# Norms in two steps, the pooling tied behind the mixing, and the recurrence's scans spread over the LRU gate

## The chip, the cores and the metric

The program runs on one core of a Trainium2 chip. The metric is the device time of one execution in microseconds (us): the time before is the median of three runs, 1450.72 us (1448.88 to 1451.69). The engines are TensorE (PE), VectorE (DVE), ScalarE (ACT), GpSimd (POOL) and SyncE (SP). Each works through its own instructions strictly in their order; semaphores tie the engines together.

## The reference

A batch of one, 256 tokens by 1024 features, float32, goes through two blocks. The first has two layers; each merges three branches of one input projection: a gated MLP with a spatial mix, an attention with low-rank queries and keys, and a gated linear recurrence (RG-LRU, 1280 channels). The second block has a pooling mixer and then a sparse attention, each followed by a convolutional FFN (2816 wide) and a gated per-layer embedding (PLE). What matters here:

```python
# RG-LRU, in each layer of the first block
a = jnp.exp(-8.0 * r * softplus(-lam))              # r, i: sigmoid gates of the convolved input xc
mult = jnp.sqrt(jnp.maximum(1.0 - a * a, 0.0))
h = scan(a, mult * i * xc)                          # h[t] = a[t]*h[t-1] + b[t] along the 256 tokens
y_c = h * silu(z_c)
merged = (sigmoid(g_a) * (y_a @ w_proj_a) + sigmoid(g_b) * (y_b @ w_proj_b)
          + sigmoid(g_c) * (y_c @ w_proj_c))
x = x + rmsnorm(merged @ w_out, post_norm_g)        # the next layer starts with rmsnorm(x)
# second block, layer 0
x = x + pool_mixer(rmsnorm(x), pool_w, pool_scale)  # average over the last 2, 4, 8, 16 tokens, minus the token, times a matrix
x = x + conv_ffn(rmsnorm(x))
x = x + sigmoid(rmsnorm(x) @ ple_gate) * (p @ ple_proj)   # then the norms for keys and values, attention, FFN, PLE
```

## The kernel before, in words

**Weights.** All weights are streamed once, in a fixed order, in chunks of up to 128x1024 floats: SP's queue loads a chunk into `raw` (4 buffers), ScalarE copies it, rounded to fp32r, into `hi` (L376), VectorE subtracts to get the remainder `lo` (L379, two instructions of 128x512), and TensorE multiplies. A product of two split operands is three matmuls, `mm3` (L481, L482, L483): in the rows `psA<-hi,hT` is weight chunk hi with the split input hT. There are 7 buffers of hi and lo, and a chunk is split two chunks ahead of its use in the program.

**Tokens.** They lie as two halves of 128 partitions, `x[0]` and `x[1]` (`x_70`, `x_71` in the rows), each 128x1024. A norm (`norm`, L543) sums squares of the two 512-wide quarters on ScalarE (`junk`, L512), adds them on VectorE (`ms`, L501), takes the power -1/2 on GpSimd (`rs`, L502), scales the quarters on VectorE (`tmp`, L526), or first multiplies by the gain where the factor is folded in later, transposes on TensorE (L538, into psB) and splits the transposed tile on ScalarE (hi, L488) and VectorE (lo, L489) into `hT`, the input of the next matrix. TensorE can't start the next matrix before that.

**The LRU gate.** In `first_layer` the recurrence's coefficients `av` are done, on ScalarE, before the branch gate `gc` is computed (two column halves n, four chunks each, from L894). The block from L982 to L994 then squares av (L985), takes the minimum with 1 (L986), the root on ScalarE (L987, with its own table), multiplies (L989) and scans along the tokens (L992). The next matrix is zc: five pairs, each one gated into `yc` (L1001, L491, L492), then the matrix pc, which reads yc.

**The residuals.** `tok_pair` (L579) multiplies both halves with the 8 chunks of a 1024x1024 matrix (wo here, pg in `ple`): six chunks are held, so that half 0 ends before half 1 does. Only after the whole call does the program write the residual and the norm of half 0 and then of half 1; for wo (L1012 to L1020) `t` is the product times a gain, and x gets t times rs. `ffn` does the same behind its `down` matrix. `pool` (L1071) averages with a matrix `pm` in psB (`pooled`, L1089), splits into `uf`, and mixes (`mixed`, L1096).

**Order.** The program is written engine by engine in the order of these Python calls; a list scheduler with costs of its own then fixes the order of each engine, by the readiness that it computes, and adds semaphore waits. That order doesn't change at run time.

Of the kernel before, what the change touches and what calls it, by code (L numbers as in the profile page):

```python
# [12 lines left out]
AF = mybir.ActivationFunctionType  # L13
ALU = mybir.AluOpType
AX = mybir.AxisListType

P = 128
S = 256
D = 1024
KD = D // P  # L20
# [16 lines left out]
KF = D_FF // P  # L37
# [148 lines left out]
FFN_LAG = 8  # L186
NSA_ORDER = (("kv", 1), ("kv", 2), ("q", 0), ("cmp", 0), ("cmp", 1), ("gt", 0))
FFN_TAIL = 7
PAIR_HELD = 6
SPECS = _specs()  # L190
W_TOTAL = sum(n for _, n, _ in SPECS) * P
# [227 lines left out]
class Net:  # L419
# [59 lines left out]
    def mm3(self, ps, a, b, start, stop):  # L479
        mm = self.nc.tensor.matmul  # L480
        mm(ps, a[0], b[0], start=start, stop=False)  # L481
        mm(ps, a[0], b[1], start=False, stop=False)  # L482
        mm(ps, a[1], b[0], start=False, stop=stop)  # L483

    def split(self, hi, lo, src, scale=None):
        nc = self.nc
# [56 lines left out]
    def norm(self, *key, dst=None, rs=None, fold=None):  # L543


        gain = self.row(*key)
        dst = dst or self.feat4("hT", KD)
        run_rs = rs or [None, None]

        def run(half):  # L550
            if fold:
                hs = self.u2s("h", 2)
                for n, h in enumerate(hs):
                    cs = slice(n * 512, (n + 1) * 512)
                    self.nc.vector.tensor_tensor(h, self.x[half][:, cs], gain[n], op=ALU.mult)
            if run_rs[half] is None:
                run_rs[half] = self.rs_x(half, fold or 1.0)
            if not fold:
                hs = self.scaled_x(half, run_rs[half], gain)
            for n, h in enumerate(hs):  # L560
                self.transpose_split(h, dst, half, 4 * n, 4)

        run.dst, self.rs = dst, run_rs
        return run

# [10 lines left out]
                self.mm3(ps[half][:, :N], f.pair(kg, half), (wh[:, k, :], wl[:, k, :]), kg == 0, kg == kts - 1)  # L576
            yield ps[half]

    def tok_pair(self, key, f):  # L579

        ps = [[self.psA(), self.psA()] for _ in range(2)]
        def part(half, i, w):
            n, c = divmod(i, 4)
            for k in range(2):
                kg = 2 * c + k
                self.mm3(ps[n][half], f.pair(kg, half), (w[0][:, k, :], w[1][:, k, :]), kg == 0, kg == KD - 1)

        def get(i):
            return self.w.get((*key, i // 4, i % 4), 512)

        ws = [get(i) for i in range(PAIR_HELD)]
        for i in range(PAIR_HELD):
            part(0, i, ws[i])
        for i in range(8 - PAIR_HELD):
            part(1, i, ws[i])
            ws.append(get(PAIR_HELD + i))
            part(0, PAIR_HELD + i, ws[-1])
        for i in range(8 - PAIR_HELD, 8):
            part(1, i, ws[i])
        return ps  # L600

    def feat_tile(self, ps, key, f, kts=KD, k0=0, tot=None):
# [130 lines left out]
    def first_layer(self, l):  # L733
# [241 lines left out]
        for kind, i in MERGE_ORDER:  # L975
            if kind == "a":
                project("pa", i, ya, 8, gate("ga", i))
            else:
                gates(i)
        tg = [gate("gc", n) for n in range(2)]  # L980
        tv = self.u2s("tv", 5)
        quarter = self.small(1, "quarter", 2)  # L982
        nc.vector.tensor_scalar(quarter, av[4][:, :1], 0.0, 0.25, op0=ALU.mult, op1=ALU.add)
        for j in range(5):
            nc.vector.tensor_tensor(tv[j], av[j], av[j], op=ALU.mult)  # L985
            nc.vector.tensor_scalar(tv[j], tv[j], 1.0, None, op0=ALU.min)  # L986
            nc.scalar.activation(tv[j], tv[j], AF.Sqrt, bias=quarter, scale=-0.25)  # L987
        for j in range(5):
            nc.vector.tensor_tensor(xc[j], xc[j], tv[j], op=ALU.mult)  # L989
            for e in range(2):  # L990
                ct = 2 * j + e
                nc.vector.tensor_tensor_scan(ctile(av, ct), ctile(av, ct), ctile(xc, ct), 0.0,  # L992
                                             op0=ALU.mult, op1=ALU.add)
        if l == 1:  # L994
            self.ple_load(0)
            self.w.scale = self.row("pscale")
        yc = self.feat2("yc", KL)
        for j in range(5):
            sz = self.tmp()
            self.silu2(sz, self.feat_pair(("zc", l), hT, j))  # L1000
            nc.vector.tensor_tensor(sz, av[j], sz, op=ALU.mult)  # L1001
            self.split(*yc.span(2 * j, 2), _k3(sz, S), 0.5)

# [5 lines left out]
                self.transpose_split(merged[half][n], ms, half, 4 * n, 4, 0.5)  # L1009
        g_post = self.row("post", l)  # L1010
        nxt = self.norm("pre", 1) if l == 0 else self.pool_norm()
        pss = self.tok_pair(("wo", l), ms)  # L1012
        for half in range(2):
            ts = self.u2s("t", 2)
            for n in range(2):
                nc.vector.tensor_tensor(ts[n], pss[n][half], g_post[n], op=ALU.mult)
            r = self.rs_of([pss[0][half], pss[1][half]], D)
            for n in range(2):
                xs = self.x[half][:, n * 512:(n + 1) * 512]
                nc.vector.scalar_tensor_tensor(xs, ts[n], r, xs, op0=ALU.mult, op1=ALU.add)  # L1020
            nxt(half)
        self.hT = nxt.dst

    def mla_head(self, h, qT, kT, qrT, krT, vt, szb, yb):
# [46 lines left out]
    def pool(self):  # L1071
        nc = self.nc
        h = self.hT
        pms = [self.sp.tile([P, 1024], F32, tag=t, name="pm", bufs=HL_BUFS) for t in ("hi", "lo")]
        for i in range(2):
            nc.scalar.dma_start(pms[i], self.aps["pm"][:, i * 1024:(i + 1) * 1024])
        pm = [p.rearrange("p (g k t) -> p g k t", g=2, k=2) for p in pms]
        self.ple_in(0, 0)
        self.rope_tables()
        w = [self.w.get(("pool", gp), S) for gp in range(2)]  # L1080
        nxt = self.norm("ffn", 0)
        uf = self.feat4("uf", 8)
# [12 lines left out]

        def mixed(half):  # L1096
            for gp in range(2):
                wh, wl = w[gp]
                cs = slice(gp * 512, gp * 512 + 512)
                ps = self.psA()  # L1100
                for e in range(2):
                    for k in range(2):
                        self.mm3(ps[:, e * S:(e + 1) * S], uf.pair(4 * gp + 2 * e + k, half),
                                 (wh[:, 2 * e + k, :], wl[:, 2 * e + k, :]), k == 0, k == 1)
                nc.vector.tensor_tensor(self.x[half][:, cs], self.x[half][:, cs], ps, op=ALU.add)

        pooled(0, 0)
        pooled(1, 0)
        mixed(0)
        pooled(1, 1)  # L1110
        nxt(0)
        mixed(1)
        nxt(1)
        self.hT = nxt.dst

    def ffn(self, l):
# [5 lines left out]
        act = {}  # L1122

        def up(j):
# [16 lines left out]
            self.split(f[:, 0, :], f[:, 1, :], c[:, :S])  # L1141
            act[j] = f

        def down(*js):
            ws = [self.w.get(("down", l, j), 512) for j in js]
            for half in range(2):
                sl = slice(half * P, half * P + P)
                for j, (wh, wl) in zip(js, ws):
                    f = act[j]
                    for n in range(2):  # L1150
                        self.mm3(acc[half][n], (f[:, 0, sl], f[:, 1, sl]), (wh[:, n, :], wl[:, n, :]),
                                 j == 0, j == KF - 1)

        for j in range(KF):
            up(j)
# [2 lines left out]
        for j in range(KF - FFN_LAG, KF - FFN_TAIL):  # L1158
            down(j)
        nxt = self.norm("ple", l, fold=0.5)  # L1160
        down(*range(KF - FFN_TAIL, KF))
        for half in range(2):
            for n in range(2):
                cs = slice(n * 512, (n + 1) * 512)
                nc.vector.tensor_tensor(self.x[half][:, cs], self.x[half][:, cs], acc[half][n], op=ALU.add)  # L1165
            nxt(half)
        self.hT = nxt.dst

    def ple_load(self, l):
# [14 lines left out]
    def ple(self, l):  # L1184
        nc = self.nc
        hT, rs = self.hT, self.rs
        if l == 0:
            self.ple_load(1)
        nxt = self.norm("nkv", fold=1.0) if l == 0 else self.final()
        pss = self.tok_pair(("pg", l), hT)  # L1190
        for half in range(2):
            for n in range(2):
                cs = slice(n * 512, n * 512 + 512)
                t = self.tmp()
                nc.scalar.activation(t, pss[n][half], AF.Tanh, scale=rs[half])
                nc.vector.scalar_tensor_tensor(t, t, 1.0, self.pp[half][n], op0=ALU.add, op1=ALU.mult)
                nc.vector.tensor_tensor(self.x[half][:, cs], self.x[half][:, cs], t, op=ALU.add)
            nxt(half)
        self.hT = nxt.dst

    def rope_nsa(self, x, tab, nh, n):
# [331 lines left out]
```

## Time and profile before

| | us |
|---|---|
| median of 3 runs | 1450.72 |
| profiled execution | 1449.2 |
| its span in the trace | 1447.4 |
| TensorE busy | 1406.5 (97%) |
| VectorE busy | 1059.7 (73%) |
| ScalarE busy | 842.0 (58%) |
| GpSimd busy | 73.2 (5%) |

The span is that of the trace; the execution has 1.8 us more around it. The share of TensorE, 97%, is a mean: it is nearly 100% within the matrices, and lower where the program goes from one matrix to the next through a norm or a gate. The mean granted clock of TensorE is 0.996 of full speed. A matmul's own duration in a row is longer than the distance to the next one, since they are pipelined.

### The profile page before, as it was taken

How to read it: one execution, taken by the hardware profiler on the slowest of the kernel's cores; microseconds unless marked ns; L12 is line 12 of the kernel's file. 1: busy time of each engine (PE TensorE's matmuls, PEld its weight loads, DVE VectorE, ACT ScalarE, POOL GpSimd, SP SyncE). 2: the span in 40 equal slices, each digit the busy share in tenths (PEclk: the TensorE clock that was granted, in tenths of full speed). 3: DMA queues.
4: the chain of work that ended last, by engine and by line, in shares of the span. 5: the costliest groups of instructions: out<-in, count | busy, mean ns of one | idle time of the engine just before them, and what ended most of it. 6: DMA issues, size and time to landing. Idle time of an engine off the chain costs nothing.

```text
span 1447.4 us, 23030 instructions
## 1 busy us (share of the span) xinstructions
PE 1406.5 (97%) x8522; PEld 1235.7 (85%) x8522; DVE 1059.7 (73%) x2163; ACT 842.0 (58%) x1411; POOL 73.2 (5%) x118
## 2 busy tenths in 40 slices
PE   6999999999999999999999999999999999999997
PEld 6987889889789878898897899999778677999986
DVE  7856748659677567486597788776795888787765
ACT  6665545656465665456564566554665786665553
POOL 1000002100010000021000000000100120000000
PEclk9999999999999999999999999999999999999999
DMA  8563456554655634555656455555453106655552
GB/s 281 182 195 117 166 183 196 170 202 149 218 161 195 197 117 159 190 187 170 211 178 218 150 201 178 190 186 193 167 181 131 59 15 191 194 184 189 187 162 90
DMA packets 73408, 249.32 MB, mean 172 GB/s; under 512 B 8272, under 2 KB 8912, under 8 KB 73296
## 3 DMA queue, kind: packets, MB, share of 16 engines
q1 hardware_dynamic: 72576, 245.95, 51.9%
q10 hardware_dynamic: 720, 1.91, 0.4%
q8 instruction: 67, 1.10, 0.3%
q14 instruction: 45, 0.37, 0.1%
HBM read 246.77 MB, written 1.05 MB: 171 GB/s over the span
## 4 chain that ended last, share of the span: by engine, by line
PE 81%; DVE 9%; DMA 4%; ACT 3%; issue 2%; POOL 1%; POOLq 0%; ACTq 0%; DVEq 0%; SPq 0%
PE psA L481 22%; PE psA L482 22%; PE psA L483 22%; DMA raw<-in_w_dram 3%; PE psB L481 3%; PE psB L482 3%; PE psB L483 3%; DVE lo L379 3%; ACT hi L376 2%; PE psB L538 1%; DVE av L992 1%; POOL rs L502 1%; PE psB L1036 1%; PE psB L1054 1%; PE psB L1422 1%
## 5 line engine op out<-in xcount | busy, mean ns | idle before, releaser
L379 DVE TENSOR_TENSOR lo<-raw,hi 128x512 fp32r<-128x512 f32 (+2 forms) x897 | 583.9, 677 | 217.4 <-ACT hi L376 212.0
L376 ACT ACTIVATE hi<-raw 128x1024 fp32r<-128x1024 f32 (+3 forms) x449 | 466.7, 1044 | 310.6 <-PE psA L483 110.3
L482 PE MATMUL psA<-hT,hi 128*128 128x256 f32 x1160 | 328.6, 283 | 0.5 <-DVE hT L489 0.5
L483 PE MATMUL psA<-hT,lo 128*128 128x256 f32 x1160 | 328.2, 283 | 0.0
L481 PE MATMUL psA<-hT,hi 128*128 128x256 f32 x1160 | 328.2, 283 | 0.0
L481 PE MATMUL psA<-hi,hT 128*128 128x512 f32 (+2 forms) x592 | 230.5, 390 | 3.9 <-ACT hT L488 3.9
L482 PE MATMUL psA<-lo,hT 128*128 128x512 f32 (+2 forms) x592 | 228.6, 386 | 1.6 <-DVE lo L379 1.6
L483 PE MATMUL psA<-hi,hT 128*128 128x512 f32 (+2 forms) x592 | 229.1, 388 | 0.0
L482 PEld LDWEIGHTS psA<-hT,hi 128*128 128x128 f32 x1160 | 221.9, 191 | 2.0 <-DVE hT L489 0.7
L481 PEld LDWEIGHTS psA<-hT,hi 128*128 128x128 f32 x1160 | 221.8, 191 | 1.5 <-ACT hT L488 0.2
L483 PEld LDWEIGHTS psA<-hT,lo 128*128 128x128 f32 x1160 | 222.0, 191 | 0.0
L481 PEld LDWEIGHTS psA<-hi,hT 128*128 128x128 f32 x592 | 111.5, 188 | 24.1 <-ACT hT L488 4.9
L482 PEld LDWEIGHTS psA<-lo,hT 128*128 128x128 f32 x592 | 111.4, 188 | 21.9 <-DVE lo L379 2.3
L483 PEld LDWEIGHTS psA<-hi,hT 128*128 128x128 f32 x592 | 111.4, 188 | 20.6 <-DVE hT L489 0.7
L1135 DVE SCALAR_TENSOR_TENSOR tmp<-psA,colt,tmp 128x255 f32<-128x255 f32 (+1 forms) x176 | 84.1, 478 | 1.2
L502 POOL TENSOR_TENSOR rs<-ms,mhalf 128x1 f32<-128x1 f32 x34 | 28.9, 851 | 979.2 <-DVE ms L501 790.6
L481 PE MATMUL psB<-hi,fact 128*128 128x512 f32 x176 | 68.8, 391 | 0.0
L482 PE MATMUL psB<-lo,fact 128*128 128x512 f32 x176 | 68.8, 391 | 0.0
L483 PE MATMUL psB<-hi,fact 128*128 128x512 f32 x176 | 68.5, 389 | 0.0
L1132 ACT ACTIVATE tmp<-psA,colt 128x256 f32<-128x256 f32 x88 | 48.5, 551 | 1.9
L512 ACT ACTIVATE junk<-x 128x512 bf16<-128x512 f32 x36 | 22.6, 628 | 36.3 <-DVE x L1165 14.0
L936 POOL CAST es<-xs 64x256 fp32r<-64x256 f32 x48 | 29.4, 640 | 270.1 <-ACT xs L488 269.3
(343 smaller groups left out, 2235.0 us busy)
## 6 DMA issues: line engine op xcount, KB each, us to landing
raw<-in_w_dram SPq DMA_DIRECT2D x414, 512.0 KB, 3.7
raw<-in_w_dram SPq DMA_DIRECT2D x24, 384.0 KB, 3.9
row<-in_rows_dram SPq DMA_DIRECT2D x34, 256.0 KB, 5.6
raw<-in_w_dram SPq DMA_DIRECT2D x8, 448.0 KB, 3.2
raw<-in_w_dram SPq DMA_DIRECT2D x4, 480.0 KB, 3.3
x<-in_x_dram SPq DMA_DIRECT2D x4, 256.0 KB, 4.6
pm<-in_pm_dram ACTq DMA_DIRECT2D x2, 512.0 KB, 5.3
out_dram<-h SPq DMA_DIRECT2D x4, 256.0 KB, 2.1
```

The source lines that it names most:

```text
L376: self.nc.scalar.activation(hi[:, :n], t[:, :n], AF.Copy)
L379: self.nc.vector.tensor_tensor(lo[:, c], t[:, c], hi[:, c].bitcast(F32), op=ALU.subtract)
L481: mm(ps, a[0], b[0], start=start, stop=False)
L482: mm(ps, a[0], b[1], start=False, stop=False)
L483: mm(ps, a[1], b[0], start=False, stop=stop)
L502: nc.gpsimd.tensor_tensor(rs, ms, self.mhalf, op=ALU.pow)
L512: nc.scalar.activation(junk[:, :s.shape[1]], s, AF.Square, scale=float(n) ** -0.5 / mul, accum_out=ss[:, i:i + 1])
L538: nc.tensor.transpose(ps[:, i, :], src[:, (done + i) * P:(done + i + 1) * P], self.cf("ident"))
L936: nc.gpsimd.tensor_copy(edges[p][m][i][r], xs.pair(ct)[i][r].bitcast(F32))
L992: nc.vector.tensor_tensor_scan(ctile(av, ct), ctile(av, ct), ctile(xc, ct), 0.0, op0=ALU.mult, op1=ALU.add)
L1132: nc.scalar.activation(dst, src, AF.Identity, bias=self.col("fb", ct, l), scale=self.col("fw", 2 * 2 * KF + ct, l))
L1135: nc.vector.scalar_tensor_tensor(dst[:, s:], src[:, :S - s], self.col("fw", (2 - s) * 2 * KF + ct, l), dst[:, s:], op0=ALU.mult, op1=ALU.add)
```

## The change

Five edits. (1) At the LRU gate the squares go from VectorE to ScalarE, the minimum from VectorE to GpSimd, and the five steps of multiply and scan are called one by one: j=0 after the first half of gate gc, j=1 after the second, j=2 to 4 inside the first three pairs of zc. (2) A norm's `run` is cut into `scale` (sums, rs, scaled quarters) and `turn` (transposes and split), and callers place the two. (3) `tok_pair` calls the residual of half 0 before half 1's last chunks; for pg the transposes of half 0 are tied, by `issue_after`, behind the fourth of half 1's last six chunks; for wo in layer 0 both `turn` calls come after the whole matrix. (4) In `pool` the pooling of half 1 is tied behind the last product of the mixing of half 0, and half 0's transposes behind the mixing of half 1. (5) In `ffn` half 0's transposes are tied behind the third last j of half 1's down products. Line numbers after the change are 2 higher up to `split`, and 19 to 53 higher from `first_layer` to `ple`.

```diff
@@ norm
-        def run(half):
+        hs = [None, None]
+        def scale(half):
             if fold:
-                hs = self.u2s("h", 2)
...
             if not fold:
-                hs = self.scaled_x(half, run_rs[half], gain)
-            for n, h in enumerate(hs):
+                hs[half] = self.scaled_x(half, run_rs[half], gain)
+        def turn(half):
+            for n, h in enumerate(hs[half]):
                 self.transpose_split(h, dst, half, 4 * n, 4)
+        def run(half):
+            scale(half)
+            turn(half)
@@ tok_pair
             part(0, PAIR_HELD + i, ws[-1])
+        if first:
+            first(0, [ps[0][0], ps[1][0]])
         for i in range(8 - PAIR_HELD, 8):
-            part(1, i, ws[i])
+            ins = part(1, i, ws[i])
+            if turn and i == 8 - PAIR_HELD + PAIR_LATE - 1:
+                with self.tc.issue_after(ins):
+                    turn(0)
+        if first:
+            first(1, [ps[0][1], ps[1][1]])
@@ first_layer
-        tg = [gate("gc", n) for n in range(2)]
...
         for j in range(5):
-            nc.vector.tensor_tensor(tv[j], av[j], av[j], op=ALU.mult)
-            nc.vector.tensor_scalar(tv[j], tv[j], 1.0, None, op0=ALU.min)
+            nc.scalar.activation(tv[j], av[j], AF.Square)
+            nc.gpsimd.tensor_scalar(tv[j], tv[j], 1.0, 1.0, op0=ALU.min, op1=ALU.mult)
+        for j in range(5):
             nc.scalar.activation(tv[j], tv[j], AF.Sqrt, bias=quarter, scale=-0.25)
-        for j in range(5):
+        def scan(j):
             nc.vector.tensor_tensor(xc[j], xc[j], tv[j], op=ALU.mult)
...
+        tg = [gate("gc", 0)]
+        scan(0)
+        tg.append(gate("gc", 1))
+        scan(1)
...
             self.silu2(sz, self.feat_pair(("zc", l), hT, j))
+            if j < 3:
+                scan(j + 2)
...
-        pss = self.tok_pair(("wo", l), ms)
-        for half in range(2):
+        def residual(half, pss):
...
-            nxt(half)
+            if l == 0:
+                nxt.scale(half)
+            else:
+                nxt(half)
+        self.tok_pair(("wo", l), ms, residual)
+        if l == 0:
+            for half in range(2):
+                nxt.turn(half)
@@ pool
-        mixed(0)
-        pooled(1, 1)
-        nxt(0)
-        mixed(1)
+        last = mixed(0)
+        nxt.scale(0)
+        with self.tc.issue_after(last):
+            pooled(1, 1)
+        last = mixed(1)
+        with self.tc.issue_after(last):
+            nxt.turn(0)
         nxt(1)
@@ ffn
+        for half in range(2):
+            for j, w in zip(js, ws):
+                ins = down_one(j, half, w)
+                if half and j == KF - FFN_LATE:
+                    with self.tc.issue_after(ins):
+                        nxt.turn(0)
+            residual(half)
+        nxt.turn(1)
@@ ple
-            nxt(half)
+            if l == 0:
+                nxt.scale(half)
+            else:
+                nxt(half)
+        self.tok_pair(("pg", l), hT, residual, nxt.turn if l == 0 else None)
+        if l == 0:
+            nxt.turn(1)
```

VectorE at the LRU gate of layer 0, before; L968 is the last step on the gated input, L379 a weight remainder, L618 the first step of zc:

```order
L968 SCALAR_TENSOR_TENSOR xc<-tmp,xc 128x256 x3
L379 TENSOR_TENSOR lo<-raw,hi 128x512 x18
L985 TENSOR_TENSOR tv<-av 128x512 x2
L986 TENSOR_SCALAR tv<-tv 128x512 x2
L985 TENSOR_TENSOR tv<-av 128x512 x2
L986 TENSOR_SCALAR tv<-tv 128x512 x2
L985 TENSOR_TENSOR tv<-av 128x512
L989 TENSOR_TENSOR xc<-xc,tv 128x512
L986 TENSOR_SCALAR tv<-tv 128x512
L992 SCALAR_TENSOR_TENSOR av<-av,xc 128x256 x2
L989 TENSOR_TENSOR xc<-xc,tv 128x512 x2
L992 SCALAR_TENSOR_TENSOR av<-av,xc 128x256 x4
```

The same place now (L987 is the gated input, L381 the remainder, L1009 the multiply, L1012 the scan, L637 the first step of zc):

```order
L987 SCALAR_TENSOR_TENSOR xc<-tmp,xc 128x256 x3
L381 TENSOR_TENSOR lo<-raw,hi 128x512
L1009 TENSOR_TENSOR xc<-xc,tv 128x512 x2
L1012 SCALAR_TENSOR_TENSOR av<-av,xc 128x256 x4
L1009 TENSOR_TENSOR xc<-xc,tv 128x512 x2
L381 TENSOR_TENSOR lo<-raw,hi 128x512 x2
L1012 SCALAR_TENSOR_TENSOR av<-av,xc 128x256 x4
L1009 TENSOR_TENSOR xc<-xc,tv 128x512
L381 TENSOR_TENSOR lo<-raw,hi 128x512 x8
L1012 SCALAR_TENSOR_TENSOR av<-av,xc 128x256 x2
L381 TENSOR_TENSOR lo<-raw,hi 128x512 x13
L637 SCALAR_TENSOR_TENSOR tmp<-tmp,psA 128x512
```

The chain stood behind 18 remainders, those of gate gc among them; it now stands ahead of all but one of them, and the remainders of gc n=1 stand between its parts.

ScalarE from wo to the next norm in layer 0, before (hT<-psB is the split of a transposed quarter, junk<-psA a sum of squares of half 1's product, junk<-x_71 one of the new x):

```order
L376 ACTIVATE hi<-raw 128x640
L488 ACTIVATE hT<-psB 128x4x128
L512 ACTIVATE junk,ss<-psA 128x512
L488 ACTIVATE hT<-psB 128x4x128
L512 ACTIVATE junk,ss<-psA 128x512
L512 ACTIVATE junk,ss<-x_71 128x512 x2
```

The same place now:

```order
L378 ACTIVATE hi<-raw 128x640
L514 ACTIVATE junk,ss<-psA 128x512 x2
L490 ACTIVATE hT<-psB 128x4x128
L514 ACTIVATE junk,ss<-x_71 128x512
L490 ACTIVATE hT<-psB 128x4x128
L514 ACTIVATE junk,ss<-x_71 128x512
```

Both sums of half 1's product come ahead of half 0's split, and its second quarter stands behind a sum over the new x_71.

VectorE at that place, before (hT<-psB the remainder of a transposed quarter, x_71<-t,rs,x_71 the residual of half 1):

```order
L1016 TENSOR_TENSOR t<-psA,row 128x512 x2
L379 TENSOR_TENSOR lo<-raw,hi 128x512
L489 TENSOR_TENSOR hT<-psB,hT 128x4x128
L379 TENSOR_TENSOR lo<-raw,hi 128x448
L489 TENSOR_TENSOR hT<-psB,hT 128x4x128
L501 TENSOR_SCALAR ms<-ss 128x1
L379 TENSOR_TENSOR lo<-raw,hi 128x512
L1020 SCALAR_TENSOR_TENSOR x_71<-t,rs,x_71 128x512 x2
```

The same place now:

```order
L1043 TENSOR_TENSOR t<-psA,row 128x512 x2
L381 TENSOR_TENSOR lo<-raw,hi 128x512
L381 TENSOR_TENSOR lo<-raw,hi 128x448
L503 TENSOR_SCALAR ms<-ss 128x1
L381 TENSOR_TENSOR lo<-raw,hi 128x512
L1047 SCALAR_TENSOR_TENSOR x_71<-t,rs,x_71 128x512 x2
L491 TENSOR_TENSOR hT<-psB,hT 128x4x128 x2
```

Both remainders of half 0's hT have moved behind the two residuals of half 1.

## Rows read from the trace of the kernel before

**Rows 1.** The page's first part: busy us, share of the span, instructions.

```profile
PE 1406.5 (97%) x8522; PEld 1235.7 (85%) x8522; DVE 1059.7 (73%) x2163; ACT 842.0 (58%) x1411; POOL 73.2 (5%) x118
```

**Rows 2.** TensorE's waits: line, releaser, us in total, times, longest.

```profile
PE psA L481 <- ACT hT L488: 3.9, 4, 1.2
PE psA L481 <- ACT yc L491: 3.3, 3, 1.7
PE psB L1089 <- DVE tmp L526: 2.7, 1, 2.7
...
PE psA L483 <- DVE yc L492: 0.8, 2, 0.4
```

**Rows 3.** Windows: us, busy PE PEld DVE ACT POOL, PEclk, DMA share, GB/s.

```profile
763.60:767.10 3.50, 3.50 (x10) 2.73 (x9) 2.06 (x4) 0.63 (x1) 0.00 (x0) 0.51 0.80 267
821.60:825.10 3.50, 3.34 (x15) 3.34 (x16) 3.16 (x6) 1.66 (x3) 0.00 (x0) 0.51 0.87 263
```

**Rows 4.** Timeline of TensorE, pooling on: start us, us, instruction, [idle before <-releaser].

```profile
821.76 2.93 PE L1089 MATMUL psB<-pm,tmp 128*128 128x128 f32 x12 [2.71 <-DVE tmp L526]
...
835.65 1.38 PE L538 MATMUL psB<-cft,tmp 128*128 128x128 f32 x8 [1.16 <-DVE tmp L526]
```

**Rows 5.** Instructions of tile tv: ns min/median/max, first and last start.

```profile
L985 DVE TENSOR_TENSOR tv<-av x10: 681/684/686, 328.4 to 731.2; 128x512 f32<-128x512 f32 x10
L986 DVE TENSOR_SCALAR tv<-tv x10: 417/419/421, 329.6 to 732.4; 128x512 f32<-128x512 f32 x10
...
L989 DVE TENSOR_TENSOR xc<-xc,tv x10: 660/678/684, 332.7 to 738.0; 128x512 f32<-128x512 f32 x10
```

**Rows 6.** Timeline of VectorE, the end of the block, layer 0.

```profile
339.56 2.42 DVE L992 TENSOR_TENSOR_SCAN av<-av,xc 128x256 f32<-128x256 f32 x4
```

**Rows 7.** Timeline of TensorE at the end of zc, layer 0.

```profile
363.85 0.50 PE L481 MATMUL psA<-hi,yc 128*128 128x512 f32 x1 [1.66 <-ACT yc L491]
```

**Rows 8.** Timeline of ScalarE from wo to the next norm, layer 0.

```profile
413.41 0.58 ACT L488 ACTIVATE hT<-psB 128x512 fp32r<-128x512 f32 x1
413.89 0.59 ACT L512 ACTIVATE junk<-psA 128x512 bf16<-128x512 f32 x1
```

**Rows 9.** Timeline of ScalarE at the LRU gate, layer 0.

```profile
306.36 1.21 ACT L967 ACTIVATE tmp<-psA,lrub 128x256 f32<-128x256 f32 x3
...
329.54 1.28 ACT L987 ACT_TABLE_LOAD   x1
330.83 2.57 ACT L987 ACTIVATE tv<-tv,quarter 128x512 f32<-128x512 f32 x4
```

**Rows 10.** Instructions of line 1412 on GpSimd.

```profile
L1412 POOL TENSOR_SCALAR es<-es,sm x32: 369/475/1162, 1124.6 to 1190.1; 128x128 f32<-128x128 f32 x16, 128x256 f32<-128x256 f32 x16
```

**Rows 11.** Timeline of TensorE in gate gc, layer 0, ten products apart.

```profile
317.57 0.39 PE L481 MATMUL psA<-hi,hT 128*128 128x512 f32 x1
...
319.84 0.39 PE L482 MATMUL psA<-lo,hT 128*128 128x512 f32 x1
```

**Rows 12.** Timeline of TensorE from wo to the next norm, layer 0.

```profile
411.71 1.29 PE L538 MATMUL psB<-cft,tmp 128*128 128x128 f32 x8 [0.46 <-DVE tmp L526]
414.04 0.44 PE L481 MATMUL psA<-hi,hT 128*128 128x384 f32 x1 [1.04 <-ACT hT L488]
...
421.24 0.63 PE L538 MATMUL psB<-cft,tmp 128*128 128x128 f32 x4 [0.78 <-DVE tmp L526]
```

**Rows 13.** Timeline of VectorE from wo to the next norm, layer 0.

```profile
417.01 1.42 DVE L1020 SCALAR_TENSOR_TENSOR x<-t,rs,x 128x512 f32<-128x512 f32 x2 [0.44 <-POOL rs L502]
```

**Rows 14.** Timeline of VectorE in the pooling.

```profile
820.96 1.41 DVE L526 SCALAR_TENSOR_TENSOR tmp<-x,rs,row 128x512 f32<-128x512 f32 x2 [0.45 <-POOL rs L502]
822.29 0.68 DVE L489 TENSOR_TENSOR uf<-psB,uf 128x512 fp32r<-128x512 f32 x1
```

**Rows 15.** Timeline of TensorE after ffn 0 and after ple 0.

```profile
1026.99 0.50 PE L481 MATMUL psA<-hi,hT 128*128 128x512 f32 x1 [1.24 <-ACT hT L488]
...
1051.31 0.50 PE L481 MATMUL psA<-hi,hT 128*128 128x512 f32 x1 [0.47 <-ACT hT L488]
```

More of the change, by code (lines that the diff above doesn't have):

```diff
@@ L188 @@
 FFN_TAIL = 7
+FFN_LATE = 3
+PAIR_LATE = 4
 PAIR_HELD = 6
@@ L482, in mm3 @@
         mm(ps, a[0], b[1], start=False, stop=False)
-        mm(ps, a[1], b[0], start=False, stop=stop)
+        return mm(ps, a[1], b[0], start=False, stop=stop).ins
     def split(self, hi, lo, src, scale=None):
@@ L548, in norm @@
         run_rs = rs or [None, None]
-        def run(half):
+        hs = [None, None]
+        def scale(half):
             if fold:
-                hs = self.u2s("h", 2)
-                for n, h in enumerate(hs):
+                hs[half] = self.u2s("h", 2)
+                for n, h in enumerate(hs[half]):
                     cs = slice(n * 512, (n + 1) * 512)
@@ L558, in run @@
             if not fold:
-                hs = self.scaled_x(half, run_rs[half], gain)
-            for n, h in enumerate(hs):
+                hs[half] = self.scaled_x(half, run_rs[half], gain)
+        def turn(half):
+            for n, h in enumerate(hs[half]):
                 self.transpose_split(h, dst, half, 4 * n, 4)
+        def run(half):
+            scale(half)
+            turn(half)
+        run.scale, run.turn = scale, turn
         run.dst, self.rs = dst, run_rs
@@ L577, in tok_halves, with tok_pair @@
             yield ps[half]
-    def tok_pair(self, key, f):
+    def tok_pair(self, key, f, first=None, turn=None):
         ps = [[self.psA(), self.psA()] for _ in range(2)]
@@ L585, in part @@
                 kg = 2 * c + k
-                self.mm3(ps[n][half], f.pair(kg, half), (w[0][:, k, :], w[1][:, k, :]), kg == 0, kg == KD - 1)
+                ins = self.mm3(ps[n][half], f.pair(kg, half), (w[0][:, k, :], w[1][:, k, :]), kg == 0, kg == KD - 1)
+            return ins
         def get(i):
@@ L1011, in first_layer @@
         nxt = self.norm("pre", 1) if l == 0 else self.pool_norm()
-        pss = self.tok_pair(("wo", l), ms)
-        for half in range(2):
+        def residual(half, pss):
             ts = self.u2s("t", 2)
             for n in range(2):
-                nc.vector.tensor_tensor(ts[n], pss[n][half], g_post[n], op=ALU.mult)
-            r = self.rs_of([pss[0][half], pss[1][half]], D)
+                nc.vector.tensor_tensor(ts[n], pss[n], g_post[n], op=ALU.mult)
+            r = self.rs_of(pss, D)
             for n in range(2):
@@ L1102, in mixed @@
                     for k in range(2):
-                        self.mm3(ps[:, e * S:(e + 1) * S], uf.pair(4 * gp + 2 * e + k, half),
-                                 (wh[:, 2 * e + k, :], wl[:, 2 * e + k, :]), k == 0, k == 1)
+                        ins = self.mm3(ps[:, e * S:(e + 1) * S], uf.pair(4 * gp + 2 * e + k, half),
+                                       (wh[:, 2 * e + k, :], wl[:, 2 * e + k, :]), k == 0, k == 1)
                 nc.vector.tensor_tensor(self.x[half][:, cs], self.x[half][:, cs], ps, op=ALU.add)
+            return ins
         pooled(0, 0)
         pooled(1, 0)
-        mixed(0)
-        pooled(1, 1)
-        nxt(0)
-        mixed(1)
+        last = mixed(0)
[5 more added lines that the diff above has]
+            nxt.turn(0)
         nxt(1)
@@ L1142, in up, with down_one @@
             act[j] = f
+        def down_one(j, half, w):
+            sl, f = slice(half * P, half * P + P), act[j]
+            for n in range(2):
+                ins = self.mm3(acc[half][n], (f[:, 0, sl], f[:, 1, sl]), (w[0][:, n, :], w[1][:, n, :]),
+                               j == 0, j == KF - 1)
+            return ins
         def down(*js):
@@ L1146, in down @@
             for half in range(2):
[L1147 to L1152, printed above, removed]
+                for j, w in zip(js, ws):
+                    down_one(j, half, w)
         for j in range(KF):
@@ L1160, in ffn, with residual @@
         nxt = self.norm("ple", l, fold=0.5)
-        down(*range(KF - FFN_TAIL, KF))
-        for half in range(2):
+        def residual(half):
             for n in range(2):
@@ L1165, in ffn @@
                 nc.vector.tensor_tensor(self.x[half][:, cs], self.x[half][:, cs], acc[half][n], op=ALU.add)
-            nxt(half)
+            nxt.scale(half)
+        js = range(KF - FFN_TAIL, KF)
+        ws = [self.w.get(("down", l, j), 512) for j in js]
+        for half in range(2):
+            for j, w in zip(js, ws):
+                ins = down_one(j, half, w)
[4 more added lines that the diff above has]
+        nxt.turn(1)
         self.hT = nxt.dst
@@ L1189, in ple, with residual @@
         nxt = self.norm("nkv", fold=1.0) if l == 0 else self.final()
-        pss = self.tok_pair(("pg", l), hT)
-        for half in range(2):
+        def residual(half, pss):
             for n in range(2):
@@ L1194, in ple @@
                 t = self.tmp()
-                nc.scalar.activation(t, pss[n][half], AF.Tanh, scale=rs[half])
+                nc.scalar.activation(t, pss[n], AF.Tanh, scale=rs[half])
                 nc.vector.scalar_tensor_tensor(t, t, 1.0, self.pp[half][n], op0=ALU.add, op1=ALU.mult)
                 nc.vector.tensor_tensor(self.x[half][:, cs], self.x[half][:, cs], t, op=ALU.add)
-            nxt(half)
+            if l == 0:
+                nxt.scale(half)
+            else:
[3 more added lines that the diff above has]
+            nxt.turn(1)
         self.hT = nxt.dst
```

## The prediction

> **What bounds the kernel now.** Read the engine table first: TensorE is busy 1406.5 of 1447.4 us [rows 1], so nothing but its holes can be won, and every edit is priced by the hole it closes or opens. Next read who makes TensorE wait: 3.9 us for the first split of a normalized input (ACT hT), 3.3 and 0.8 us for the gated recurrence (yc), 2.7 us for the pooling's scaled input [rows 2]. Then find the halved clock: two stretches of 3.5 us at a granted 0.51, which is the lower of the two levels, 1.2 GHz [rows 3]. The first follows the waits for yc in layer 1, the second the wait in the pooling; each loses at most 3.5 x 0.49 = 1.7 us. The places that the change touches hold these waits and little else, so the most it can return is 3.9 + 4.1 + 2.7, plus 1.2 at the second norm of the pooling [rows 4] and at most 3.4 of clock: near 15 us.
>
> **The LRU gate, both layers.** Removed from VectorE per layer: 5 squares of 0.684 and 5 minima of 0.419 us, 5.5 us of busy time [rows 5], a little less from start to start. They stood in one block from 328.4 to 341.98, 13.6 us in which VectorE made no weight remainder (lo) [rows 5, 6]. TensorE ran on through what was split ahead; the block came back as 1.66 us for yc at 363.85 and half of the 0.8 of [rows 2], 2.06 us in layer 0 [rows 7]. Layer 1 keeps the rest of the two waits, 4.1 - 2.06 = 2.04, and 1.7 of clock: 3.7.
>
> Now the chain stands 20 us earlier. ScalarE finishes the last tanh at 306.36 + 1.21 = 307.57, then 5 Squares, which I price by its Square over 128x512 at 0.59 less the overlap of neighbours, 0.55 each (to 310.3) [rows 8], a table load of 1.28, then Sqrt at 0.62 spacing [rows 9]: the first result at 312.3, the second at 312.9. GpSimd's 5 minima are new. The nearest row is its TENSOR_SCALAR on smaller tiles, 0.477 us mean, least 0.369, longest 1.162 [rows 10]. I extend the two small forms to about 0.7, as an estimate; even at 1.16 the first two are through before the Sqrts take them, so they cost 0, at most 0.5 us. VectorE waits for the Sqrts with its weight splits queued behind: two multiplies from 312.4, four half-scans, two multiplies (0.60 each, as [rows 6] has 2.42 for four) end near 317.4; the second chunk of gate gc n=1 is split by 318.6, just as TensorE wants it; four more scans and a multiply end at 321.5; only then comes the third chunk's lo, ready at 322.1. TensorE wants that chunk's second product at 319.84 [rows 11]: a new wait of 2.3 us, between 1.5 (Sqrts 0.8 sooner) and 2.8. The two remaining scans and the last pairs of zc fit, as a pair gives VectorE 7 steps of 0.60, 4.2 us, and TensorE 24 products of 0.227 [rows 11], 5.4 us. In layer 1 the loads for PLE also stand two weight loads earlier on SP; no wait of TensorE in [rows 2] is for a load, so I price that at 0. Layer 0: 2.3 - 2.06 = +0.2. Layer 1: 2.3 - 3.7 = -1.4. If the block hides wholly, both ends are -2.06 and -3.7; if the clock falls behind the new wait, add 1.7 each.
>
> The row on the table load also decides a point of the Trainium skill. The load takes 1.28 us and the first Sqrt starts 0.01 us after its end [rows 9]. "ScalarE: Activation LUTs", section "What ACT_TABLE_LOAD costs", adds a drain of about 1.38 us to each switch, 2.66 in all. By the row the wait is 2.3, by the page 3.7 in each layer; the measurement decides (rival D).
>
> **From wo to the next norm, layer 0.** The old waits are 0.46, 1.04 and 0.78: 2.28 us [rows 12]. ScalarE copied half 0's hT at 413.41, before half 1's two sums of squares [rows 8]. Now these two come first (0.59 each, [rows 8]), so the copy starts at 414.6 and TensorE's first product near 415.25. The second hT copy stands behind a sum over x_71, which waits for the residual on VectorE, and VectorE does both hT remainders after the two residuals of half 1. These start when GpSimd's rs is there, 417.01 before [rows 13], and about 1.1 us sooner without the two remainders ahead (2 x 0.60): 415.9 to 417.35. The remainder is at 418.05, where the third product needs it. TensorE's hole: transposes end at 413.0, four products (0.7 us) run, and work resumes at 418.05: 4.35 us instead of 1.04. Half 1's transposes, now 20 products earlier, still find their input late (VectorE scales it from about 419.65), 0.6 us. Sum 0.46 + 4.35 + 0.6 = 5.4, so +3.1; best case 2.28 gone, worst 1.7 of clock on top: -2.3 to +4.8. Layer 1's wo runs to the pooling as before.
>
> **Pooling.** TensorE waits 2.71 us for the scaled x_71 [rows 4], which VectorE makes at 820.96 to 822.29, then the remainder of the pooled half 0 [rows 14]. In the new order the pooling of half 1 is tied behind the last product of the mixing of half 0. The third mixing product needs the remainder of 822.29 to 822.97: the hole is 819.05 to 822.97, 3.9 instead of 2.7, and the pooling products that stood inside come later. Some of that is returned, since the low clock falls partly in the hole. The last hole, 1.16, stays: VectorE still scales half 1 behind the residual. I take +1.3, between -0.5 (the late pooling hides the scaling of x_70) and +3.5 (8 pooling products at the 2.93 for 12 of [rows 4], 2.0, plus 1.5 of clock).
>
> **FFN to PLE, PLE to the next norm.** The holes are 1.24 after ffn 0 [rows 15], 1.15 after ffn 1 (what is left of the four waits of 3.9 in [rows 2] after 1.04, 1.24 and 0.47), and 0.47 after ple 0 plus shorter hitches. Half 0's transposes now stand 12 products of 0.227, 2.7 us, before the end, and the copy needs 1.0 after them, so these holes go. Half 1's transposes come 8 products (1.8 us) into the next matrix and wait about 0.25. I take -0.95, -0.95 and -0.8; at least 0, since only the order changes.
>
> **Sum.** 0.2 - 1.4 + 3.1 + 1.3 - 0.95 - 0.95 - 0.8 = +0.5 us on the profiled 1449.2: 1449.7. That run is 1.5 under the median of the three, 1450.7, so its equivalent is 1451.2; I state 1450.5, between both.
>
> **The rivals.**
> (A) The change does what it says: norms and scans hide. For it: VectorE loses 11 us of work over both layers and the transposes have matmuls around them. Against it: both waits above are of VectorE's and ScalarE's queue order, which the new order makes longer. It gives -2.06 - 3.7 at the gates, -1 at wo, -1 at the pooling, -2.7 at FFN and PLE: -10.5, about 1440; with half of that, 1445.
> (B) Slower, and decided by the clock: the hole at wo (4.35 us in two parts) is longer than the pooling's 2.71, behind which the clock fell [rows 3, 4]. If holes that long cost the lower level there and at one of the two gates, each adds 1.7, and with the hole at the pooling 1 us longer the sum is 0.5 + 3.4 + 1 = +5: 1455. It decides once TensorE's hole at wo passes 2.7. Against it: layer 0's 2.06 for yc left the clock at full.
> The Trainium skill says the same of the mechanism: "TensorE: Matmul & The Clock Gate", section "HAM oscillation — how this bites in real kernels", has the clock fall after waits between groups of matmuls. Here it fell after 2.04 and 2.71, and not after 2.06.
> (C) The minima on GpSimd are the bound: 1.16 us each and more while VectorE works beside them, the fifth at 314.5 instead of 311.5. The gate's chain moves back only by 0.5 to 1.5 us a layer: about 1452.
> (D) Each change of ScalarE's table costs a second time the load's 1.28 before the first Sqrt: the chain is late by 1.3 in each layer, 0.5 + 2.6 = +3.1, 1452.3. The 0.01 us behind the load in [rows 9] speaks against it. The Trainium skill's drain, named at the gate, would be such a cost.
>
> **How the numbers follow.** My sum 0.42, A 0.32, B 0.20, C 0.05, D 0.01. A difference under 0.2% (2.9 us) is about what a measurement here can't tell from none. My sum by itself holds 1446.5 to 1454, and gives 0.06 faster, 0.32 same, 0.04 slower; A 0.29 faster, 0.03 same; B 0.18 slower, 0.02 same; C and D 0.04 slower, 0.02 same. Rounded: faster 0.35, same 0.39, slower 0.26. Both signs hold much, so the range takes in A's middle and B: 1441 to 1457.
>
> **What would show it.** Right at the gate: a wait of about 2.3 us for lo near 320 and 719, none for yc after. At wo: TensorE idle over 4 us between 413 and 418, released by VectorE's hT remainder. At the pooling: one wait near 3.9 for the remainder of uf. Wrong: no wait over 1 us at wo (then A), granted clock at 0.5 near 418 or 322 (then B), the Sqrts spaced at over 1 us by GpSimd (then C).

## The result, and the profile after

The changed kernel is slower: 1460.94 us (median of 4 runs, 1459.91 to 1461.73) against 1451.2 of the kernel before (4 runs); ratio 1.0076, interval 1.0063 to 1.0089. The profiled execution took 1459.91 us, its span 1458.1. The forecast was 1450.5, between 1441 and 1457, with slower at 0.26.

The first part of the page after, which answers to [rows 1], and then TensorE's list of waits after (line, releaser, us in total, times, longest), which answers to [rows 2]:

```profile
PE 1411.1 (97%) x8522; PEld 1239.2 (85%) x8522; DVE 1053.6 (72%) x2143; ACT 848.4 (58%) x1421; POOL 93.9 (6%) x128
```

```profile
PE psA L483 <- ACT hi L378: 7.2, 4, 2.4
PE psA L485 <- DVE uf L491: 4.3, 3, 3.9
PE psA L484 <- DVE lo L381: 4.1, 6, 1.3
PE psA L483 <- ACT hT L490: 2.1, 1, 2.1
PE psA L485 <- DVE hT L491: 1.9, 1, 1.9
```

The waits for yc are gone, as forecast, and three of the four for the first split of a norm. In their place TensorE waits 7.2 + 4.1 us for weights (hi and lo), which before held it for 1.6 in all, and GpSimd has gained 20.7 us of work for ten instructions (93.9 against 73.2). The tile of the block, after (ns least/median/largest, first and last start), with the two rows on who waited:

```profile
L1003 ACT ACTIVATE tv<-av x10: 657/662/670, 307.5 to 718.6; 128x512 f32<-128x512 f32 x10
L1004 POOL TENSOR_SCALAR tv<-tv x10: 1915/2210/2355, 308.3 to 725.9; 128x512 f32<-128x512 f32 x10
...
  POOL tv L1004: 9.4, 8
```

A minimum takes 2.21 us, not the 0.7 that I had extended from [rows 10]. Eight of the ten Sqrts waited for one. ScalarE's timeline at the gate of layer 0 (columns as in [rows 9]) shows where this went:

```profile
307.48 2.75 ACT L1003 ACTIVATE tv<-av 128x512 f32<-128x512 f32 x5
310.24 1.28 ACT L1006 ACT_TABLE_LOAD   x1
311.54 0.72 ACT L1006 ACTIVATE tv<-tv,quarter 128x512 f32<-128x512 f32 x1
312.58 0.72 ACT L1006 ACTIVATE tv<-tv,quarter 128x512 f32<-128x512 f32 x1 [0.32 <-POOL tv L1004]
314.80 0.73 ACT L1006 ACTIVATE tv<-tv,quarter 128x512 f32<-128x512 f32 x1 [1.50 <-POOL tv L1004]
...
319.15 0.72 ACT L1006 ACTIVATE tv<-tv,quarter 128x512 f32<-128x512 f32 x1 [1.46 <-POOL tv L1004]
319.77 1.04 ACT L378 ACTIVATE hi<-raw 128x1024 fp32r<-128x1024 f32 x1
```

Up to the first Sqrt the forecast holds to 0.1 us (Squares to 310.24, table load 1.28, Sqrt at 311.54 where I had 311.6). From the second on the Sqrts come 2.2 us apart, which is the sign that the prediction had named for rival C. The next weight copy (hi) stands behind the fifth: 319.77, where [rows 11] has TensorE already at the third chunk of this half of gc. TensorE's waits there:

```profile
320.87 0.49 PE L483 MATMUL psA<-hi,hT 128*128 128x512 f32 x1 [2.40 <-ACT hi L378]
321.59 0.50 PE L484 MATMUL psA<-lo,hT 128*128 128x512 f32 x1 [0.23 <-DVE lo L381]
324.21 0.50 PE L483 MATMUL psA<-hi,hT 128*128 128x512 f32 x1 [1.18 <-ACT hi L378]
325.73 0.50 PE L484 MATMUL psA<-lo,hT 128*128 128x512 f32 x1 [1.02 <-DVE lo L381]
```

So it is ScalarE's copy that is late, through GpSimd, more than VectorE's remainder. Behind these holes, and behind those at wo, the granted clock falls (windows as in [rows 3]):

```profile
324.00:328.00 4.00, 2.77 (x8) 2.04 (x9) 4.00 (x8) 3.00 (x4) 0.00 (x0) 0.82 0.40 138
328.00:332.00 4.00, 4.00 (x15) 3.19 (x14) 3.34 (x7) 1.55 (x2) 0.00 (x0) 0.76 0.86 291
...
422.00:426.00 4.00, 3.10 (x10) 3.10 (x11) 3.49 (x7) 1.50 (x5) 0.86 (x1) 0.51 0.26 60
426.00:430.00 4.00, 4.00 (x19) 3.83 (x18) 1.85 (x5) 1.20 (x2) 0.00 (x0) 0.63 0.94 321
```

From wo to the next norm, TensorE after (answers to [rows 12]), then ScalarE, then VectorE:

```profile
416.72 1.29 PE L540 MATMUL psB<-cft,tmp 128*128 128x128 f32 x8 [0.42 <-DVE tmp L528]
420.08 0.44 PE L483 MATMUL psA<-hi,hT 128*128 128x384 f32 x1 [2.08 <-ACT hT L490]
422.90 0.69 PE L485 MATMUL psA<-hi,hT 128*128 128x384 f32 x1 [1.91 <-DVE hT L491]
```

```profile
418.87 0.59 ACT L514 ACTIVATE junk<-psA 128x512 bf16<-128x512 f32 x1
...
419.44 0.60 ACT L490 ACTIVATE hT<-psB 128x512 fp32r<-128x512 f32 x1
```

```profile
420.83 1.41 DVE L1047 SCALAR_TENSOR_TENSOR x<-t,rs,x 128x512 f32<-128x512 f32 x2 [0.44 <-POOL rs L504]
422.17 1.44 DVE L491 TENSOR_TENSOR hT<-psB,hT 128x512 fp32r<-128x512 f32 x2
```

The two holes, 2.08 and 1.91, stand where the forecast put them and are 4.0 long where it said 4.35; the copy of hT is behind the second sum, its remainder behind the residual of half 1. In the pooling TensorE, after, against [rows 4]:

```profile
834.00 0.39 PE L485 MATMUL psA<-hi,uf 128*128 128x256 f32 x1 [3.93 <-DVE uf L491]
...
849.43 1.29 PE L540 MATMUL psB<-cft,tmp 128*128 128x128 f32 x8 [1.71 <-DVE tmp L528]
```

The price of each place can be taken from the two traces: the starts of the same matmul, counted from the first, are compared ahead of a place and behind it.

| place | forecast, us | after against before, us |
|---|---|---|
| gate, layer 0 and layer 1 | +2.3, +2.3 | +7.6, +6.0 |
| waits for yc, layer 0 and layer 1 | -2.06, -3.7 | -2.6, -4.8 |
| wo to norm, layer 0 | +3.1 | +4.9 |
| pooling with its norm | +1.3 | +2.6 |
| FFN 0 to PLE, PLE 0 to norm, FFN 1 to PLE | -0.95, -0.8, -0.95 | -1.8, -0.9, -1.1 |
| attention | 0 | +0.8 |
| all | +0.5 | +10.7 |

The +0.8 in the attention is one more stretch at the lower clock (granted 0.50 from 1183.3 to 1186.7); across it the changed kernel falls back by 1.6 us against the same matmuls of before.

### The profile page after: what moved, and what is told of

The parts are those of the page before. It is cut to its first block, busy times and chain, and to the rows that moved or that the text cites. A ratio compares the mean times of both kernels' runs of the same rounds, so it can differ in the third digit from the quotient of the medians.

```text
span 1458.1 us, 23043 instructions
## 1 busy us (share of the span) xinstructions
PE 1411.1 (97%) x8522; PEld 1239.2 (85%) x8522; DVE 1053.6 (72%) x2143; ACT 848.4 (58%) x1421; POOL 93.9 (6%) x128
## 3 DMA queue, kind: packets, MB, share of 16 engines
q10 hardware_dynamic: 720, 1.91, 0.4%
## 4 chain that ended last, share of the span: by engine, by line
PE 85%; DVE 6%; ACT 3%; issue 2%; POOL 2%; DMA 2%; POOLq 0%; ACTq 0%; DVEq 0%
PE psA L484 23%; PE psA L485 23%; PE psA L483 23%; PE psB L483 3%; PE psB L484 3%; PE psB L485 3%; DVE lo L381 2%; DMA raw<-in_w_dram 1%; POOL tv L1004 1%; PE psB L540 1%; ACT hi L378 1%; POOL rs L504 1%; PE psB L1089 1%; PE psB L1071 1%; PE psB L1482 1%
## 5 line engine op out<-in xcount | busy, mean ns | idle before, releaser
L381 DVE TENSOR_TENSOR lo<-raw,hi 128x512 fp32r<-128x512 f32 (+2 forms) x897 | 586.0, 678 | 221.2 <-ACT hi L378 216.3
```

The costliest lines, as they stand in the source:

```text
L381: self.nc.vector.tensor_tensor(lo[:, c], t[:, c], hi[:, c].bitcast(F32), op=ALU.subtract)
```

## The experiments

Ratios are to the kernel before, run beside each; 0.001 of it is 1.45 us. The theory after the traces, G: GpSimd's minima, 2.2 us each, make most of the new wait at the gate. Its rival, Q: the scans' place ahead of the weight remainders on VectorE makes it, however fast the minima are.

**e1, the minimum on VectorE.**

```diff
-            nc.gpsimd.tensor_scalar(tv[j], tv[j], 1.0, 1.0, op0=ALU.min, op1=ALU.mult)
+            nc.vector.tensor_scalar(tv[j], tv[j], 1.0, None, op0=ALU.min)
```

> The changed kernel with one edit: the minimum on VectorE instead of GpSimd; the order of all else is the same. Theory G (each GpSimd minimum of 2.2 us spaces the Sqrts, and the chain that follows holds back the weight splits): the gate now costs about 2.3 us instead of 7.6 in layer 0 and 6.0 in layer 1, so 9 us less, about 1452. Rival Q (the scans stand ahead of the weight remainders on VectorE, and that alone makes the wait, however fast the minima are): the gate still costs 6 us or more in each layer, 1458 to 1461.

1451.99 us, ratio 1.0019 (1.0008 to 1.0029). The gate costs 3.8 and 2.15 us by the same matmuls, instead of 7.6 and 6.0: 3.8 us less in each layer, 7.6 in all. G holds. Layer 0's 3.8 is above the expected 2.3 because of the clock: behind the one wait there, TensorE ran at 0.51 from 323.8 to 327.2, and in layer 1, behind the same wait, at 1.00. So both pairs compare like with like: layer 0 has one such stretch in both kernels, layer 1 has none in either. VectorE's timeline in e1, and TensorE's one wait:

```profile
309.67 1.90 DVE L1004 TENSOR_SCALAR tv<-tv 128x512 f32<-128x512 f32 x5
...
319.14 2.42 DVE L1012 TENSOR_TENSOR_SCAN av<-av,xc 128x256 f32<-128x256 f32 x4
321.49 0.66 DVE L1009 TENSOR_TENSOR xc<-xc,tv 128x512 f32<-128x512 f32 x1
322.07 4.89 DVE L381 TENSOR_TENSOR lo<-raw,hi 128x512 fp32r<-128x512 f32 x8
```

```profile
322.81 0.50 PE L484 MATMUL psA<-lo,hT 128*128 128x512 f32 x1 [1.86 <-DVE lo L381]
```

The chain of the forecast is here to the letter, 0.9 us later as a whole in this run: second chunk split, four scans, multiply, third chunk's remainder, and TensorE waiting for just that. I had 2.3 us; the wait is 1.86, and layer 1, with the clock at full, loses 2.15. So with minima of a harmless length the forecast for the gate stands, and Q is what is left of the wait.

**e2, the gate as before in the changed kernel** (the block of [rows 5] and the scans back behind gate gc).

```diff
-            nc.scalar.activation(tv[j], av[j], AF.Square)
-            nc.gpsimd.tensor_scalar(tv[j], tv[j], 1.0, 1.0, op0=ALU.min, op1=ALU.mult)
+            nc.vector.tensor_tensor(tv[j], av[j], av[j], op=ALU.mult)
+            nc.vector.tensor_scalar(tv[j], tv[j], 1.0, None, op0=ALU.min)
...
-            if j < 3:
-                scan(j + 2)
```

> The changed kernel with the LRU gate of the kernel before (squares, minima, scans on VectorE after gate gc); everything else as changed. If the gate is the largest part of the loss: 7.6 + 6.0 - 2.6 - 4.8 = 6.2 us less, 1454.7. If the loss lies mostly in the norms and the pooling and the gate only moves the wait: less than 3 us, 1458 or more.

1454.17 us, ratio 1.0027 (1.0017 to 1.0036): 7.1 us less than the changed kernel by the ratios. The gate is the largest part of the loss.

**e3, the residual and norm behind wo as before.**

```diff
-        self.tok_pair(("wo", l), ms, residual)
-        if l == 0:
-            for half in range(2):
-                nxt.turn(half)
+        pss = self.tok_pair(("wo", l), ms)
+        for half in range(2):
...
+            nxt(half)
```

> The changed kernel with the residual and norm behind wo as before, both layers. If the 4.9 us lost between wo and the next matrix in layer 0 come from the new order there (ScalarE's and VectorE's splits behind half 1's sums and residual, and the low clock that follows): 4.9 less, 1456.0. If the low clock there is left over from the wait at the gate upstream: 2 to 3 less, 1458.

1456.36 us, ratio 1.0051 (1.0036 to 1.0066): 3.6 less by the ratios, 4.2 at the place itself (0.8 left of 4.9). Nearer to the first expectation. The 0.8 that is left goes with the clock: e3 has a granted 0.50 from 419.9 to 423.3, behind waits of 0.42 and 1.09 us in the old order, where before, e4, e7 and e8, with no new wait at the gate, have 1.00 from 405 to 430. So the second expectation may hold for this small part; e9 tests the rest.

**e4, only the edits behind the FFNs and the first PLE.**

```diff
-        last = mixed(0)
-        nxt.scale(0)
-        with self.tc.issue_after(last):
-            pooled(1, 1)
...
+        mixed(0)
+        pooled(1, 1)
+        nxt(0)
```

(with the gate of e2 and the wo of e3)

> The kernel before with only the edits behind the FFNs and the first PLE (gate, wo and pooling as before). If the places add up: 1.75 + 0.9 + 1.06 less and 0.8 more in the attention's start, so 2.9 us faster than before, 1448.3. If the changes of order there are only shifted into later waits: within 1 us of before, 1450.2 to 1452.2.

1446.45 us, ratio 0.9978 (0.9965 to 0.999): 3.2 us faster than before, as the places added up. Moving a norm's transposes among the last products pays where the input is ready in time.

**e5, the pooling's order as before** in the changed kernel (the edit to `pool` of e4 alone).

> The changed kernel with the pooling's order as before (pooled half 1 ahead of the norm of half 0, nothing tied). If the tied pooling costs what the two traces show there, 2.6 us: 1458.4. If that place only inherits the low clock or late weights from wo: within 1 us of the changed kernel, 1460 to 1462.

1459.27 us, ratio 1.0068 (1.0054 to 1.0082). The place itself costs 0 instead of 2.6, but the total shows only 1.2 to 1.7 of it. The two profiles differ elsewhere too: layer 1's gate cost 7.6 in e5's, with 3.4 us at 0.50 behind it, and 6.0 in the changed kernel's. Whether that also makes the difference of the medians isn't shown. The intervals of e5 and the changed kernel overlap, so by time alone this part is unclear.

**p1 and p2, what a GpSimd step costs.**

```diff
-            nc.gpsimd.tensor_scalar(tv[j], tv[j], 1.0, 1.0, op0=ALU.min, op1=ALU.mult)
+            nc.gpsimd.tensor_scalar(tv[j], tv[j], 1.0, None, op0=ALU.min)
```

```diff
-            nc.gpsimd.tensor_scalar(tv[j], tv[j], 1.0, 1.0, op0=ALU.min, op1=ALU.mult)
+            nc.gpsimd.tensor_scalar(tv[j], tv[j], 1.0, 1.0, op0=ALU.mult, op1=ALU.mult)
```

> The changed kernel with the minimum on GpSimd as a single operation, without the multiplication by 1. Theory (a GpSimd step costs by its number of operations): about 1.1 us instead of 2.2 for each of the ten, gate wait 3 us less. Rival (it costs by the elements, one or two operations alike): 1.9 to 2.3 us, no change.

> The changed kernel with a multiplication by 1 in place of the minimum on GpSimd, so two multiplications by 1 as line 1412 has (the guard against a value above 1 is left out). Theory (the minimum is the slow operation, as two multiplications took 0.48 us on average over tiles of 128x128 and 128x256): under 1.2 us each. Rival (128x512 costs this much with any operation here): 1.9 to 2.3 us.

The line's instructions in p1, then in p2 (ns least/median/largest):

```profile
L1004 POOL TENSOR_SCALAR tv<-tv x10: 1479/1562/1930, 308.0 to 719.0; 128x512 f32<-128x512 f32 x10
```

```profile
L1004 POOL TENSOR_SCALAR tv<-tv x10: 612/616/1051, 307.9 to 714.7; 128x512 f32<-128x512 f32 x10
```

In p1 both numbers missed: the minimum alone takes 1.56 us, between 1.1 and 1.9. In p2 the theory held: two multiplications over the same tile take 0.62. So 0.7 was a fair extension of [rows 10], but of a multiplication; the minimum is another price. p2 also bears on G: the step is still on GpSimd and the order is the changed kernel's, and TensorE's wait at the gate is that of e1, 1.9 us for lo in each layer, against 4.9 and 4.8 (hi and lo) in the changed kernel and 2.4 in p1. So it is the length of the step that counts, not that it moved. One run each: 1454.77 and 1453.00 us.

**e7, the scans tied behind zc's weight remainders**, minima on VectorE, on the base of e4.

```diff
+            self.last = self.nc.vector.tensor_tensor(lo[:, c], t[:, c], hi[:, c].bitcast(F32), op=ALU.subtract).ins
...
-            if j < 3:
-                scan(j + 2)
+            with self.tc.issue_after(self.w.last):
+                scan(j)
```

> The kernel before with the edits behind the FFNs and the first PLE (as e4) and the gate in a third form: squares on ScalarE, minima on VectorE, both early as in the change, but each multiply and scan tied behind a weight remainder of zc, so that gate gc is not held up. Theory Q2 (only the place of the scans on VectorE makes the 2.0 us wait that is left with minima on VectorE): gate within 0.6 us of before, and the waits for yc gone (2.6 and 4.8 us as in the change), so 1446.5 - 6.8 = 1439.7. Rival (VectorE is full in zc and the waits for yc come back): 1445 to 1447.

1439.95 us, ratio 0.9945 (0.9931 to 0.996), faster than both kernels. The gate costs 0.06 and 0.04 us; of the waits for yc one is left in TensorE's list:

```profile
PE psA L483 <- ACT yc L493: 0.6, 1, 0.6
```

So what was left of the wait in e1 was the place of the scans on VectorE, and most of the block's gain can be had: 2.2 and 3.6 us by the same matmuls, of the changed kernel's 2.6 and 4.8. It isn't all had in every profile: e8 and e9 below have the same gate, and TensorE waits 2.7 and 2.0 us for yc in theirs.

**e8 and e9, which part of the edit behind wo loses**, on the base of e7. In e8 the residual is early, the norm whole; in e9 the transposes of both halves come after both residuals.

```diff
-        pss = self.tok_pair(("wo", l), ms)
-        for half in range(2):
+        def residual(half, pss):
...
+        self.tok_pair(("wo", l), ms, residual)
```

```diff
-            nxt(half)
+            if l == 0:
+                nxt.scale(half)
...
+        if l == 0:
+            for half in range(2):
+                nxt.turn(half)
```

> e7 with one more edit: the residual of half 0 behind wo is written before half 1's last chunks, as in the change, but its norm runs whole at once (scale and transposes together). Theory (the loss behind wo comes from writing the transposes of both halves after both residuals, which lets half 1's sums and residual ahead of half 0's splits): no loss here, 1438.5 to 1440.5, the same as e7 or 1 us better. Rival (the earlier residual by itself makes the loss): 1443 or more.

> e8 with the transposes of both halves behind wo in layer 0 written after both residuals, as in the change, on a gate without the new wait. Theory (as for e8, and independent of the gate upstream): 4 to 5 us more than e8, 1443.5 to 1445. Rival (the loss behind wo needed the wait at the gate, by late weights or the clock): within 1 us of e8.

e8: 1439.97 us, ratio 0.9927 (0.9912 to 0.9943), so no loss against e7's 0.9945. e9: 1443.90 us, ratio 0.9953 (0.9938 to 0.9967). The late transposes cost 3.9 us with no wait at the gate upstream, just under the 4 to 5 expected. TensorE's waits from wo on in e8, then in e9:

```profile
410.27 0.63 PE L540 MATMUL psB<-cft,tmp 128*128 128x128 f32 x4 [1.37 <-DVE tmp L528]
420.25 0.63 PE L540 MATMUL psB<-cft,tmp 128*128 128x128 f32 x4 [1.01 <-DVE tmp L528]
```

```profile
410.79 1.29 PE L540 MATMUL psB<-cft,tmp 128*128 128x128 f32 x8 [0.46 <-DVE tmp L528]
414.13 0.44 PE L483 MATMUL psA<-hi,hT 128*128 128x384 f32 x1 [2.06 <-ACT hT L490]
416.95 0.69 PE L485 MATMUL psA<-hi,hT 128*128 128x384 f32 x1 [1.91 <-DVE hT L491]
```

The pair of 2.06 and 1.91 is the changed kernel's, 2.08 and 1.91, to 0.02 us: it follows from the order alone. What follows the pair doesn't: the lower clock lasts 3.4 us in e9 and 6.8 in the changed kernel.

## Why the prediction was wrong

- **The step that failed is the price of GpSimd's minima**: "I extend the two small forms to about 0.7, as an estimate; even at 1.16 the first two are through before the Sqrts take them, so they cost 0, at most 0.5 us." They take 2.21 us and cost 3.8 us in each layer (e1), 7.6 of the 10.2 us by which the sum was short. The row came from another operation: p2 shows 0.62 for that one on this very tile. Rival C had the mechanism, but a price of 0.5 to 1.5 us a layer and a chance of 0.05. The bound of 1.16 was the longest row of the wrong operation, so it bounded nothing. And the forecast had only VectorE's splits behind the Sqrts; ScalarE's own weight copy stood behind the fifth.
- **The rest of the gate was right.** With the minima off GpSimd, e1 shows the wait of 2.3 us as 1.86, at the chunk and the product named; the 1.6 us of clock behind it in layer 0 is within the 1.7 that the prediction named beside its sum. The waits for yc went, 2.6 and 4.8 where 2.06 and 3.7 stood.
- **wo was right in its mechanism and short in one term.** The holes are 2.08 + 1.91 (forecast 4.35), and the 0.6 for half 1's transposes didn't come: with the 0.42 ahead of them TensorE waits 4.4 us, 2.1 more than before, where the forecast had 5.4 and 3.1. The rest of the 4.9, 2.8 us by difference, goes with the low clock behind the holes, 0.51 and 0.63 in the eight us after. The forecast had it at 1.7, in its worst case and rival B alone, not in the sum. In e8, without these two holes, the window from 405 to 425 us has a granted clock of 1.00; in e9, 0.91.
- **Rival B was right about the clock**: it fell at wo and behind one of the two gates, as B had it: layer 0's (0.82 and 0.76), not layer 1's, which explains 7.6 against 6.0. B's 1455 and the 7.6 of the minima make 1462.6; measured were 1460.9. Where it falls changes from profile to profile: layer 1's gate costs 6.0 in two and 7.6 in e5.
- **The pooling** was +2.6 for +1.3, inside its bounds (-0.5 to +3.5): the hole is 3.93, as forecast, and the next norm's came to 1.71 instead of staying at 1.16. **The FFNs and the PLE** gained 3.7 for 2.7 forecast; e4 confirms the sign.
- **The table load**: the Sqrt starts 0.02 us after the load, as in [rows 9], so rival D fell. The drain that the Trainium skill adds ("ScalarE: Activation LUTs", section "What ACT_TABLE_LOAD costs") doesn't show in this trace either.
- What stays open: why the clock falls in the attention. The stretch is in the profiles of the changed kernel, e1, e5, p1 and p2, and not in those of before, e2, e3, e4, e7, e8 and e9. TensorE's list of waits for the 24 us ahead of it is the same before and after, one wait of 0.5 us; no run here separates the cause.

## What to carry to other kernels

Before work is moved to another engine, find a row of the same operation on that engine, or measure it: another operation of the same name and shape can differ by 3.6 times, as here 2.21 against 0.62 us. Work taken off a busy engine and put into a chain can end up as the wait of everything that stands behind the chain in the in-order queues, here ScalarE's weight copies; the same scans tied behind the weight splits cost 0.06 and 0.04 us (e7). And when a norm is cut in two, look at the order that comes of it: with both halves' second steps written behind both first steps, half 1's sums and residual went ahead of half 0's split here (3.9 us, e9 against e8).

## What the hardware showed that I had not expected

GpSimd's `tensor_scalar` over 128x512 float32: 0.62 us for two multiplications, 1.56 for a minimum alone, 2.21 for a minimum and a multiplication. The Trainium skill ("GPSIMD Engine Reference", section "4.1 Engine selection") calls one-input elementwise work there roughly line-rate; the multiplications come near to that, at 1.5 times the 0.42 us of VectorE's minimum in e1; GpSimd's minimum alone doesn't, at 3.7 times.

The 2.21 isn't one price for all: in both layers the second minimum, with VectorE idle for nearly all of it, took 1.92 us, and the later three, with VectorE's multiplies and scans and ScalarE's Sqrts beside them, 2.19 to 2.25; no run separates what lengthened them. VectorE itself lost little: four scans took 2.80 us during these minima, and 2.43 in e1, with GpSimd idle.

```profile
313.95 2.80 DVE L1012 TENSOR_TENSOR_SCAN av<-av,xc 128x256 f32<-128x256 f32 x4
```

```profile
314.40 2.43 DVE L1012 TENSOR_TENSOR_SCAN av<-av,xc 128x256 f32<-128x256 f32 x4
```

It is one of the four that is longer, 1.04 us instead of 0.66, and 1.03 in layer 1; the other three kept their times, and so did the two-input multiplies beside the minima (0.69 in both kernels). The Trainium skill ("GPSIMD Engine Reference", section "8. Key points") says that GpSimd shares its SBUF interfaces with VectorE and that they contend where VectorE reads two inputs. These scans and multiplies read two: the rows agree for one scan in four, and show nothing of it for the rest. On VectorE it is 0.4 us, a small part of the loss.

The clock fell in e1 behind a single wait of 1.86 us in layer 0 (0.51 from 323.8 to 327.2), and not behind the same wait, 1.87, in layer 1 (1.00 from 715 to 750). The length of a wait alone didn't tell here whether the lower clock would follow.
